# Seven-product sums formed on TensorE, another order of the last pieces, and eight slabs moved

## The chip, the cores and the metric

The kernel is one program on 1 core of one Trainium2 chip. The metric is the device time of one execution in microseconds; three executions of the kernel before had a median of 1919.31 us, from 1918.39 to 1920.64.

## What is computed

One inference step of a decoder layer, for a prompt of 1024 tokens and a group of 8 samples of 4 tokens with the same weights (1056 tokens, width 1024):

```
h     = LN0(x) * (1 + scale1) + shift1             # scale, shift, gate: silu(c) @ w_ada, six vectors per c
proj  = h @ w_in                                   # split among four mixers:
y_a   = S5 state-space scan, gelu, GLU             # "ssm"
y_b   = gated short convolution
y_c   = chunked gated delta rule
y_d   = stick-breaking attention
mixed = sum_n sigmoid(h @ w_gate_n) * (y_n @ w_branch_n)      # w_gate: 1024 x 4096
x     = LN1(alpha * x + (1 + gate1) * (mixed @ w_o))
h2    = LN0(x) * (1 + scale2) + shift2
x     = LN2(alpha * x + (1 + gate2) * ((silu(up_a) * up_b) @ w_down))
```

Inputs, outputs and norms are float32. A large product is formed from f16 halves: each operand is split into a hi and a lo part, and three products hi*hi, hi*lo and lo*hi are accumulated (`mm3`).

## The kernel before, in words

Tokens lie along the free dimension in three blocks of TB = 352 (NTB = 3; HB = 176 is half a block), the width of 1024 as KD = 8 slices on the 128 partitions. The third block carries the 32 sample tokens at its end. The work runs in stages: LN0 and modulation to `h`; projections, attention, convolution and delta rule; the gates; `mixer_out` (w_o, LN1, h2); the feed-forward network; the last down slice with LN2.

A scheduler records the kernel's instructions and fixes one static order for each engine before the program runs. It goes by priorities (streams `sup`, `br`, `lo`, `hot`, which shift an instruction's place) and by a timeline that it simulates. So lines that follow one another in the code stand interleaved with other stages on the engines, and each engine and SP's DMA queue take their instructions strictly in the fixed order.

The stretch of the change:

- `gates(2, ...)`, the third gate, is plain: for each of 8 output slices m it loads 128 x 1024 of weights (`load_w`, transfer on L142, hi split on ScalarE at L108, lo split on GpSimd at L114), forms three token blocks of 24 products `gps<-h,whl`, and beside each the 6 products `gps<-y,wbr` of the branch. ScalarE takes the tanh (`gth`, L1490), VectorE multiplies it with the branch's PSUM (L1494), GpSimd adds the result to `mix` (L1523). PSUM has three banks `gps` for this.
- Between its groups stand *slabs* (`ada_slab`): one slab is one 128-column part of `w_ada`, loaded like a gate weight, and multiplied with the silu of c in 16 tiny products (`gps<-chl,whl`) to one column of modulation `mod` (L294, L295). They are needed only from `mixer_out` on. `A2` is the number of slabs for each m of the third gate; what is left goes to the last gates, spread evenly over their four pairs.
- `ssm` is interleaved with the third gate: matrices by sines and cosines on GpSimd, transfers through HBM (`tt<-kd`, `sy<-yo`, `gx<-sy`), the scan's products (`sps`), gelu, the GLU's 48 products `sps<-yh,whl`, and the split of `y` (L108 on ScalarE, L118 on VectorE).
- `gates7(0, ...)`, the last gates, takes output slices in four pairs and uses a seven-product scheme in place of eight products of half blocks (`seven`; forms in `ORDER7`). Its inputs are slices of h and four sums and differences of slices, `Tf` (in the profile `tf`). `sums7` makes them in six units, for three token blocks and two halves of the width: in one unit 4 adds hi + lo to f32 (L1711, two on VectorE, two on GpSimd), four adds and subtractions on VectorE (L1712, L1715, L1716, L1720) and four splits (L108 on ScalarE, L116 on VectorE). Seven forms of weights are made too (`pair_weights`, L1635 to L1643 on VectorE). The slabs' lo split is on VectorE here (`LA7`, L118). PSUM has five more banks (`gps7`) once `ssm` has released its own.

The last stage goes over four pieces of tokens (`PIECES`). For each piece 8 output slices are multiplied (`gps<-ring`) and added to x (L1966; the sample part with L1971 and L1973), GpSimd sums the slices in `S` (L1547), and `norm` follows: mean by products with a constant matrix (`nps<-S,onesD`, `nps<-x,onesD`), subtract (L186), square on ScalarE (L187), variance in products (`nps<-sq,onesD`) and the root `rs` on ScalarE (L193, L194); `affine` multiplies by rs (L227) and applies gain and offset (L230 on VectorE, L232 on ScalarE). `LV2` says how many halvings of the squares are added on VectorE before the products: 3 for the first two pieces, 0 for the last two. Two DMAs write each piece out. `onesD` products are float32, and each passes TensorE several times.

## Time and profile before

| | |
|---|---|
| median of 3 executions | 1919.31 us |
| lowest, highest | 1918.39, 1920.64 us |
| the profiled execution | 1927.88 us |
| its span in the trace | 1925.8 us |
| mean granted TensorE clock | 0.961 |
| busy: TensorE, VectorE, ScalarE, GpSimd | 90, 67, 50, 50% |

The profile is of one execution that was a little longer than those timed. Its span runs from the first to the last instruction of the trace; all stage times are of that span. Busy times are of one engine; a stage whose engines are all partly idle is bound by waits between them. A granted clock of 1.0 is 2.4 GHz and 0.5 is 1.2 GHz; values between are means over a stretch.

### The profile page before, as it was taken

What the parts mean: (1) busy time and instruction counts of PE and PEld (TensorE: products, weight loads), DVE (VectorE), ACT (ScalarE), POOL (GpSimd) and SP (SyncE); (2) the same over time, 40 slices, a digit from 0 to 9 for tenths busy, and PEclk for the clock granted to TensorE, in tenths of its full rate; (3) what the DMA queues carried; (4) which work ended last, traced back from release to release, by engine and by line L of the source; (5) the groups of instructions that cost most, each with busy time, mean ns of one, the idle gap of its engine ahead of it and who ended that gap; (6) DMA issues with size and microseconds to landing.
All of it is one profiled execution on the core that took longest, in us unless ns stands there. A gap on an engine that the chain in (4) does not pass through costs nothing.

```text
span 1925.8 us, 36541 instructions
## 1 busy us (share of the span) xinstructions
PE 1734.6 (90%) x14985; PEld 1198.5 (62%) x14985; DVE 1297.0 (67%) x2161; ACT 970.8 (50%) x1796; POOL 953.9 (50%) x952
## 2 busy tenths in 40 slices
PE   7899999999899998788689899988999998999896
PEld 3466666656566665556367555556666776767675
DVE  6763777668676765386986479677467657755748
ACT  3642454465554645235664665645445644554434
POOL 1826421222354444744541553278577667675733
PEclk9999999999999999889799999989999999999999
DMA  8222220122311112313232340001121112111112
GB/s 310 75 90 64 73 59 23 49 58 54 96 50 58 62 40 98 73 41 102 77 110 77 129 137 1 1 23 44 48 64 56 48 44 65 56 37 53 50 28 91
DMA packets 63615, 130.60 MB, mean 68 GB/s; under 512 B 16408, under 2 KB 35928, under 8 KB 63192
## 3 DMA queue, kind: packets, MB, share of 16 engines
q1 hardware_dynamic: 61912, 124.07, 20.8%
q0 software_dynamic: 1536, 4.20, 0.7%
q8 instruction: 117, 1.92, 0.4%
q14 instruction: 50, 0.41, 0.1%
HBM read 117.36 MB, written 10.88 MB: 67 GB/s over the span
## 4 chain that ended last, share of the span: by engine, by line
PE 35%; DVE 26%; POOL 12%; ACT 10%; DMA 9%; issue 7%; SPq 1%; another core or an unknown queue 0%; ACTq 0%; DVEq 0%; POOLq 0%
PE gps L87 25%; DMA wraw<-in_w_up 3%; POOL wf L1631 2%; DVE x L1903 2%; POOL whl L1631 2%; DVE ring L116 2%; PE nps L87 1%; DMA wraw<-in_w_down 1%; DVE af L1869 1%; ACT wraw L1622 1%; DVE dacc L758 1%; POOL wraw L1635 1%; PE dp L87 1%; POOL wraw L1638 1%; POOL wraw L1639 1%
## 5 line engine op out<-in xcount | busy, mean ns | idle before, releaser
L87 PEld LDWEIGHTS <-whl 128*128 128x128 f16 x6992 | 623.5, 100 | 386.1 <-issue 74.9
L87 PE MATMUL gps<-h,whl 128*128 128x352 f16 (+1 forms) x4344 | 692.9, 314 | 49.0 <-ACT ct L1683 14.8
L87 PEld LDWEIGHTS <-wf 128*128 128x128 f16 x2232 | 197.7, 99 | 71.6 <-issue 13.8
L1631 POOL TENSOR_TENSOR wf<-wraw,wf 128x512 f16<-128x512 f32 (+1 forms) x102 | 122.8, 1206 | 145.8 <-ACT wf L1630 142.9
L1631 POOL TENSOR_TENSOR whl<-wraw,whl 128x512 f16<-128x512 f32 (+1 forms) x136 | 169.2, 1250 | 47.0 <-ACT whl L1630 46.8
L114 POOL TENSOR_TENSOR whl<-wraw,whl 128x1024 f16<-128x1024 f32 (+1 forms) x66 | 149.1, 2260 | 81.2 <-ACT whl L108 79.2
L105 ACT ACTIVATE wraw<-wraw 128x1024 f32<-128x1024 f32 (+2 forms) x96 | 96.4, 1005 | 127.4 <-DMA wraw<-in_w_gate 40.1
L87 PE MATMUL gps<-tf,whl 128*128 128x352 f16 (+1 forms) x1152 | 141.1, 280 | 18.6 <-ACT ct L1683 6.9
L1622 ACT ACTIVATE wraw<-wraw 128x1024 f32<-128x1024 f32 (+1 forms) x68 | 66.5, 978 | 111.0 <-DMA wraw<-in_w_up 62.2
L1630 ACT ACTIVATE whl<-wraw 128x512 f16<-128x512 f32 (+1 forms) x136 | 79.9, 589 | 78.8 <-POOL wraw L1635 34.5
L87 PE MATMUL gps<-ring,whl 128*128 128x352 f16 (+1 forms) x864 | 103.8, 276 | 13.1 <-DVE x L1903 13.1
L87 PE MATMUL gps<-y,wbr 128*128 128x352 f16 x576 | 105.4, 319 | 8.1 <-DVE gth L1771 3.8
L1680 DVE TENSOR_TENSOR ct<-ct,gps 128x352 f32<-128x352 f32 (+1 forms) x84 | 35.4, 424 | 106.5 <-PE gps L87 90.5
L1523 POOL TENSOR_TENSOR mix<-mix,gth 128x352 f32<-128x352 f32 x48 | 54.0, 1125 | 98.0 <-DVE gth L1494 87.1
L87 PE MATMUL gps<-mix,wo 128*128 128x352 f16 x576 | 88.8, 315 | 5.7 <-DVE gth L1771 3.4
L116 DVE TENSOR_TENSOR ring<-af,ring 128x352 f16<-128x352 f32 (+2 forms) x134 | 82.0, 645 | 7.8 <-ACT ring L108 7.7
L108 ACT ACTIVATE whl<-wraw 128x1024 f16<-128x1024 f32 (+1 forms) x82 | 84.8, 1035 | 4.4 <-DMA wraw<-in_w_ada 3.5
L87 PE MATMUL gps<-h,wf 128*128 128x352 f16 (+1 forms) x624 | 79.4, 283 | 6.6 <-DVE gth L1494 5.5
L87 PEld LDWEIGHTS <-wbr 128*128 128x128 f16 x576 | 56.5, 99 | 39.2 <-issue 10.2
L87 PEld LDWEIGHTS <-wo 128*128 128x128 f16 x576 | 56.7, 99 | 38.6 <-issue 5.9
L108 ACT ACTIVATE ring<-af 128x352 f16<-128x352 f32 (+2 forms) x134 | 52.2, 427 | 46.4 <-DVE af L1869 30.4
L87 PE MATMUL gps<-tf,wf 128*128 128x352 f16 (+1 forms) x528 | 66.6, 283 | 3.8 <-ACT cu L1683 3.6
(625 smaller groups left out, 3381.4 us busy)
## 6 DMA issues: line engine op xcount, KB each, us to landing
wraw<-in_w_up SPq DMA_DIRECT2D x44, 512.0 KB, 3.5
wraw<-in_w_gate SPq DMA_DIRECT2D x32, 512.0 KB, 3.9
wraw<-in_w_ada SPq DMA_DIRECT2D x32, 512.0 KB, 3.5
wraw<-in_w_in SPq DMA_DIRECT2D x20, 512.0 KB, 4.0
wraw<-in_w_down SPq DMA_DIRECT2D x24, 384.0 KB, 3.1
x<-in_xT SPq DMA_DIRECT2D x12, 704.0 KB, 7.7
araw<-in_w_ada SPq DMA_DIRECT2D x16, 512.0 KB, 10.9
wraw<-in_w_branch SPq DMA_DIRECT2D x8, 512.0 KB, 3.5
```

The source lines that it names most:

```text
L87: self.nc.tensor.matmul(out, lhsT=lhsT, rhs=rhs, start=start, stop=stop, skip_group_check=resume)
L105: nc.scalar.activation(src, src, AF.Copy, scale=scale)
L108: nc.scalar.activation(hi, src, AF.Copy, scale=scale)
L114: nc.gpsimd.tensor_tensor(lo, src, hi, op=ALU.subtract)
L116: nc.vector.tensor_tensor(lo, src, hi, op=ALU.subtract)
L758: nc.vector.scalar_tensor_tensor(acc[:, :L], ext[:, k:k + L], wts[:, i, k:k + 1], acc[:, :L], op0=ALU.mult, op1=ALU.add)
L1523: nc.gpsimd.tensor_tensor(o, o, g, op=ALU.add)
L1622: nc.scalar.activation(raw, raw, AF.Copy, scale=SW)
L1630: nc.scalar.activation(hi, src, AF.Copy)
L1631: nc.gpsimd.tensor_tensor(lo, src, hi, op=ALU.subtract)
L1680: add = lambda o, p: nc.vector.tensor_tensor(o, o, p, op=ALU.add)
L1903: nc.vector.scalar_tensor_tensor(x[:, h, z], part(h, z), gate[:, m, 0:1], x[:, h, z], op0=ALU.mult, op1=ALU.add)
```

## The change

- `sums7` is replaced for the last gates by `sums7_pe`. Four sums are formed on TensorE with a 128 x 128 identity (and its negative) in f16 as weights, the hi and lo half of h each being one product of 352 columns. A unit has 12 such products in two PSUM tiles: one for T0, the other for T3, on which T1 and then T2 are accumulated further after the split of the one before. ScalarE's hi split and VectorE's lo split read PSUM. T2 comes out with its sign turned, so its split scales by -1.
- `A2` becomes 2 and `LA7` "pool": eight slabs go from the last gates to the third gate, and the eight that stay have their lo split on GpSimd.
- The sample's block stands second in `PIECES`. The running sum `S` ends one slice earlier, and the mean takes three product terms in place of two, in LN1 and LN2. After the last piece's mean products stand 24 idle products of 352 columns, into a PSUM tile that nothing reads.

```diff
--- before.py
+++ after.py
@@ -32,9 +32,9 @@
 GSPLIT = 4
 G7 = 4
 A3 = 1
-A2 = 1
+A2 = 2
 S7 = 1
-LA7 = "dve"
+LA7 = "pool"
 R7 = (0, 2)
 QT = (0, 1, None, 2, 3, 4, 5, 6, 7)
 CORD = (6, 7, 0, 1, 8, 4, 5, 9)
@@ -44,7 +44,7 @@
 PL1 = ((0, 2), (2,))
 PL2 = (0,)
 LV2 = (3, 3, 0, 0)
-PIECES = ((0, 0, 352), (1, 0, 352), (2, 0, 192), (2, 192, 160))
+PIECES = ((0, 0, 352), (2, 0, 352), (1, 0, 192), (1, 192, 160))
 ALPHA = float(2.0 ** 0.25)
 SW = 64.0
 SA = 16.0
@@ -84,7 +84,7 @@
 
 
     def mm(self, out, lhsT, rhs, start, stop, resume=False):
-        self.nc.tensor.matmul(out, lhsT=lhsT, rhs=rhs, start=start, stop=stop, skip_group_check=resume)
+        self.last_mm = self.nc.tensor.matmul(out, lhsT=lhsT, rhs=rhs, start=start, stop=stop, skip_group_check=resume).ins
 
     def mm3(self, out, w, x, start, stop, resume=False):
         self.mm(out, w[0], x[0], start, False, resume)
@@ -157,7 +157,7 @@
         return ps
 
 
-    def norm(self, X, n, tmp, out=None, levels=3, rs_bufs=1, sq=None, tag=0, preload=True, parts=None, eps=None):
+    def norm(self, X, n, tmp, out=None, levels=3, rs_bufs=1, sq=None, tag=0, preload=True, parts=None, eps=None, warm=None):
 
         nc = self.nc
         out = X if out is None else out
@@ -185,6 +185,12 @@
         for k in (0, 4):
             nc.vector.tensor_tensor(out[:, k:k + 4], X[:, k:k + 4], bc(mean[:, None, :], (P, 4, n)), op=ALU.subtract)
             last = nc.scalar.activation(sq[:, k:k + 4], out[:, k:k + 4], AF.Square)
+        if warm:
+
+            idle = self.gtile()
+            with self.tc.issue_after(self.last_mm):
+                for i in range(warm[1]):
+                    self.mm(idle[:, :TB], warm[0][:, 0:P], warm[0][:, 0:TB], True, True)
         if preload:
             with self.tc.issue_after(last.ins):
                 nc.scalar.preload_act_table_set("natural_log_exp_and_others")
@@ -1543,7 +1549,7 @@
 
         if m == 1:
             self.nc.gpsimd.tensor_tensor(S, X[:, 0], X[:, 1], op=ALU.add)
-        elif 1 < m < KD - 1:
+        elif 1 < m < KD - 2:
             self.nc.gpsimd.tensor_tensor(S, S, X[:, m], op=ALU.add)
 
     def mixer_out(self):
@@ -1590,7 +1596,7 @@
             else:
                 dsq = pw.tile([P, 2 * KD * TB + 2 * 4 * HB], F32, name="dsq", tag="wo")
                 d, sq = dsq[:, :2 * KD * TB].rearrange("p (j k n) -> j p k n", j=2, k=KD)
-            rs = self.norm(x1, TB, tmp, sq=sq, levels=LV1[b], tag=b % 2, preload=b in PL1[0], parts=[S, x1[:, KD - 1]])
+            rs = self.norm(x1, TB, tmp, sq=sq, levels=LV1[b], tag=b % 2, preload=b in PL1[0], parts=[S, x1[:, KD - 2], x1[:, KD - 1]])
             self.affine(x1, rs, self.ln["ln1_ga"], self.ln["ln1_ba"])
             rs = self.norm(x1, TB, tmp, out=d, sq=sq, levels=LV1[b], tag=b % 2, preload=b in PL1[1], eps=self.eps_a)
             self.modulate(d, n0, TB, rs, self.mod[:, 32:40], self.mod[:, 24:32], h2[:, :, :, s])
@@ -1719,6 +1725,23 @@
                 self.split(*T(3), t3)
             nc.vector.tensor_tensor(r21, r21, r22, op=ALU.subtract)
             self.split(*T(2), r21)
+
+    def sums7_pe(self, h, Tf, b, qs):
+
+        part = lambda j, e, i: h[:, j, e::2, b * TB + i * HB:b * TB + (i + 1) * HB][:, qs]
+        T = lambda f: (Tf[:, f, 0, qs, b], Tf[:, f, 1, qs, b])
+        n = 2 * HB
+        view = lambda ps: ps.rearrange("p (q c) -> p q c", c=HB)
+        with self.sup:
+            one, two = self.gtile()[:, :n], self.gtile()[:, :n]
+            for ps, f, sgn, terms in ((one, 0, 1.0, ((0, 0, 1), (1, 0, 0))), (two, 3, 1.0, ((0, 1, 1), (1, 0, 1))),
+                                      (two, 1, 1.0, ((0, 0, 0),)), (two, 2, -1.0, ((1, 1, 0),))):
+                first = f in (0, 3)
+                for t, (neg, e, i) in enumerate(terms):
+                    for j in range(2):
+                        self.mm(view(ps), self.id16[:, neg], part(j, e, i), first and t == 0 and j == 0,
+                                t == len(terms) - 1 and j == 1, True)
+                self.split(*T(f), view(ps), sgn)
 
     @staticmethod
     def forms7(h, Tf):
@@ -1972,7 +1995,8 @@
                                                 bc(gate[:, m, 1:9, None], (P, NB, DS)), op=ALU.mult)
                         nc.vector.tensor_tensor(x[:, npr:], x[:, npr:], t, op=ALU.add)
                     self.running(S, X, m)
-            r = self.norm(X, n, tmp, levels=LV2[i], rs_bufs=2, tag=i % 2, preload=i in PL2, parts=[S, X[:, KD - 1]])
+            r = self.norm(X, n, tmp, levels=LV2[i], rs_bufs=2, tag=i % 2, preload=i in PL2, parts=[S, X[:, KD - 2], X[:, KD - 1]],
+                          warm=(act[0][:, 0], 24) if i == len(PIECES) - 1 else None)
             self.affine(X, r, self.ln["ln2_g"], self.ln["ln2_b"])
             for k in (0, 4):
                 nc.sync.dma_start(O["yT"][:, k:k + 4, s], X[:, k:k + 4])
@@ -2044,9 +2068,12 @@
     B.up_t = g7
     B.gp = B.pool("gps7", bufs=5, space=PSUM)
     Tf = g7.tile([P, 4, 2, 4, NTB, HB], F16, name="tf")
+    B.id16 = g7.tile([P, 2, P], F16, name="id16")
+    for j in range(2):
+        B.nc.vector.tensor_scalar(B.id16[:, j], B.ident, 1.0 - 2 * j, None, op0=ALU.mult)
     for b in range(NTB):
         for q in (0, 2):
-            B.sums7(B.h, Tf, b, g7.tile([P, 8 * HB], F32, name="r7", tag="r7"), slice(q, q + 2))
+            B.sums7_pe(B.h, Tf, b, slice(q, q + 2))
     B.xh7 = B.forms7(B.h, Tf)
     B.sk = B.pool("gate7w", side="right")
     B.ska = B.sk
```

Numbers of lines after the change are 6 or more higher from `norm` on (L1494 becomes L1500, L1635 L1641, L1966 L1989, L227 L233, L230 L236).

VectorE where `ssm` ends, around the splits of `y`; before, with the end of the third unit of the sums (`r_11498`) and the start of the fourth (`r_11515`):

```order
L1720 TENSOR_TENSOR r_11498<-r_11498 128x352
L118 SCALAR_TENSOR_TENSOR y<-gs,y 128x8x128
L118 SCALAR_TENSOR_TENSOR y<-gs,y 128x4x8
L116 TENSOR_TENSOR tf<-r_11498,tf 128x2x176
L1463 SCALAR_TENSOR_TENSOR gs<-gs,gx 128x1088
L295 SCALAR_TENSOR_TENSOR mod<-gps,adat 128x9
L116 TENSOR_TENSOR tf<-r_11498,tf 128x2x176 x3
L1494 SCALAR_TENSOR_TENSOR gth<-gth,gps 128x352
L118 SCALAR_TENSOR_TENSOR y<-gs,y 128x8x128
L118 SCALAR_TENSOR_TENSOR y<-gs,y 128x4x8
L1711 TENSOR_TENSOR r_11515<-h 128x352 x2
```

and now:

```order
L1469 SCALAR_TENSOR_TENSOR gs<-gs,gx 128x1088
L118 SCALAR_TENSOR_TENSOR y<-gs,y 128x8x128
L118 SCALAR_TENSOR_TENSOR y<-gs,y 128x4x8
L1469 SCALAR_TENSOR_TENSOR gs<-gs,gx 128x1088
L1500 SCALAR_TENSOR_TENSOR gth<-gth,gps 128x352
L118 SCALAR_TENSOR_TENSOR y<-gs,y 128x8x128
L118 SCALAR_TENSOR_TENSOR y<-gs,y 128x4x8
L116 TENSOR_TENSOR tf<-gps,tf 128x2x176 x3
L1641 TENSOR_TENSOR wraw<-wraw 128x4x128
L116 TENSOR_TENSOR tf<-gps,tf 128x2x176 x2
```

The adds of the sums are gone, and all the splits of the sums (`tf<-gps`) stand behind both splits of `y`, where before those of two units stood ahead of them.

SP's queue around the transfers of the scan's matrices (`kd`, `tt`) and of its state (`h<-in_st_ssm`); before:

```order
L142 DMA wraw<-in_w_gate 128x1024
L142 DMA wraw<-in_w_ada 128x1024
L1354 DMA kd<-k_10993 128x1x240 x2
L142 DMA wraw<-in_w_gate 128x1024
L1356 DMA tt<-kd 16x16x128 x8
L142 DMA wraw<-in_w_ada 128x1024
L1405 DMA h_11204<-in_st_ssm 128x128
L1418 DMA out_ssm_s<-fs 128x128
L142 DMA wraw<-in_w_gate 128x1024
L142 DMA wraw<-in_w_ada 128x1024
```

and now:

```order
L1360 DMA kd<-k_11201 128x1x240 x2
L142 DMA wraw<-in_w_gate 128x1024
L1362 DMA tt<-kd 16x16x128 x8
L142 DMA wraw<-in_w_ada 128x1024 x2
L1411 DMA h_11412<-in_st_ssm 128x128
L142 DMA wraw<-in_w_gate 128x1024
L1424 DMA out_ssm_s<-fs 128x128
L142 DMA wraw<-in_w_ada 128x1024 x2
L142 DMA wraw<-in_w_gate 128x1024
L1417 DMA out_ssm_p<-fp 128x16
L142 DMA wraw<-in_w_ada 128x1024
L1439 DMA sy<-yo_11431 16x8x136 x8
```

Each slab load (`in_w_ada`) of this stretch has become two, and one stands ahead of the transfer `sy` of the scan's result.

VectorE at the end of the program, where the 352 piece's last passes (128x1408, then 128x352) and the last piece (160 columns) meet; before:

```order
L1971 TENSOR_TENSOR gt<-gps,mod 128x32 x2
L1973 TENSOR_TENSOR x_13853<-x_13853,gt 128x32 x2
L227 TENSOR_TENSOR x_13548<-x_13548,rs 128x1408 x2
L230 TENSOR_SCALAR x_13548<-x_13548,c_ln_g,c_ln_b 128x352 x4
L186 TENSOR_TENSOR x_13853<-x_13853,nps 128x4x160 x2
L227 TENSOR_TENSOR x_13853<-x_13853,rs 128x4x192 x2
L230 TENSOR_SCALAR x_13853<-x_13853,c_ln_g,c_ln_b 128x192 x4
L227 TENSOR_TENSOR x_13853<-x_13853,rs 128x4x160 x2
L230 TENSOR_SCALAR x_13853<-x_13853,c_ln_g,c_ln_b 128x160 x4
```

and now:

```order
L172 TENSOR_TENSOR sq<-sq 128x352
L1989 SCALAR_TENSOR_TENSOR x_13597<-gps,mod,x_13597 128x160 x3
L186 TENSOR_TENSOR x_13597<-x_13597,nps 128x4x160 x2
L233 TENSOR_TENSOR x_13902<-x_13902,rs 128x1408 x2
L236 TENSOR_SCALAR x_13902<-x_13902,c_ln_g,c_ln_b 128x352 x4
L233 TENSOR_TENSOR x_13597<-x_13597,rs 128x4x192 x2
L236 TENSOR_SCALAR x_13597<-x_13597,c_ln_g,c_ln_b 128x192 x4
L233 TENSOR_TENSOR x_13597<-x_13597,rs 128x4x160 x2
L236 TENSOR_SCALAR x_13597<-x_13597,c_ln_g,c_ln_b 128x160 x4
```

The last piece's subtract with its mean (`x<-x,nps 128x4x160`) has moved ahead of the passes of the 352 piece, and the sample's instructions (`gt`) are no longer among these.

## Rows read from the trace of the kernel before

**Rows 1.** Windows by stage: us; busy us (instructions) per engine; TensorE's granted clock; DMA share; GB/s.
```profile
700.00:876.20 176.20, 148.58 (x1212) 99.63 (x1210) 97.64 (x215) 72.07 (x147) 92.46 (x85) 0.91 0.24 66
876.20:956.80 80.60, 58.60 (x425) 37.52 (x424) 70.92 (x79) 46.30 (x71) 41.29 (x30) 0.83 0.27 87
956.80:1020.00 63.20, 52.62 (x482) 38.07 (x481) 55.51 (x85) 42.68 (x85) 30.96 (x24) 0.89 0.37 118
1020.00:1069.80 49.80, 49.80 (x479) 37.16 (x476) 27.74 (x59) 22.35 (x48) 2.53 (x1) 1.00 0.16 53
```

**Rows 2.** Timeline of TensorE, 876 to 957: start, us, operation, count [idle before, releaser].
```profile
878.40 3.74 PE L87 MATMUL gps<-h,whl 128*128 128x352 f16 x24
881.98 1.06 PE L87 MATMUL gps<-y,wbr 128*128 128x352 f16 x6
...
918.58 6.66 PE L87 MATMUL gps<-h,whl 128*128 128x352 f16 x24 [5.22 <-ACT gth L1490]
...
936.15 0.89 PE L87 MATMUL gps<-h,wf 128*128 128x176 f16 x5 [5.54 <-DVE gth L1494]
```

**Rows 3.** VectorE's lines, 880 to 1080: shapes, count | busy us, mean ns | idle before.
```profile
L118 DVE SCALAR_TENSOR_TENSOR whl<-wraw,whl 128x1024 f16<-128x1024 f32 x16 | 23.3, 1456 | 0.0
...
L116 DVE TENSOR_TENSOR tf<-r,tf 128x352 f16<-128x352 f32 x24 | 16.4, 692 | 0.0
...
L1711 DVE TENSOR_TENSOR r<-h 128x352 f32<-128x352 f16 x12 | 14.1, 1214 | 0.0
...
L1712 DVE TENSOR_TENSOR r<-r 128x352 f32<-128x352 f32 x6 | 5.9, 979 | 0.0
...
L1715 DVE TENSOR_TENSOR r<-r 128x352 f32<-128x352 f32 x6 | 3.9, 646 | 0.2
...
L1716 DVE TENSOR_TENSOR r<-r 128x352 f32<-128x352 f32 x6 | 3.6, 594 | 0.0
...
L1720 DVE TENSOR_TENSOR r<-r 128x352 f32<-128x352 f32 x6 | 3.1, 517 | 0.1
```

**Rows 4.** Tile `gth`: count, ns min/median/max, first and last start, shapes.
```profile
L1494 DVE SCALAR_TENSOR_TENSOR gth<-gth,gps x48: 494/514/523, 557.5 to 946.7; 128x352 f32<-128x352 f32 x48
...
L1519 DVE TENSOR_TENSOR gth<-gth,mix x24: 510/522/2448, 982.9 to 1073.2; 128x352 f32<-128x352 f32 x24
```

**Rows 5.** Timeline of VectorE, 876 to 958.
```profile
883.67 2.89 DVE L1711 TENSOR_TENSOR r<-h 128x352 f32<-128x352 f16 x2
...
927.48 5.33 DVE L118 SCALAR_TENSOR_TENSOR y<-gs,y 128x1024 f16<-128x1024 f32 x2 [3.08 <-ACT y L108]
...
948.26 2.25 DVE L1711 TENSOR_TENSOR r<-h 128x352 f32<-128x352 f16 x2
```

**Rows 6.** TensorE's lines from 876.2, from 956.8 and from 1020, one of each.
```profile
L87 PE MATMUL sps<-yh,whl 128*128 128x272 f16 x48 | 6.6, 279 | 1.1 <-POOL whl L114 0.5 <-ACT whl L108 0.4
...
L87 PE MATMUL gps<-chl,whl 128*128 128x18 f16 x113 | 4.4, 172 | 2.6 <-DVE mod L295 2.6
...
L87 PE MATMUL gps<-chl,whl 128*128 128x9 f16 x83 | 2.8, 169 | 0.0
```

**Rows 7.** GpSimd's lines, 780 to 880.
```profile
L114 POOL TENSOR_TENSOR whl<-wraw,whl 128x1024 f16<-128x1024 f32 x8 | 17.9, 2235 | 5.1 <-ACT whl L108 5.1
```

**Rows 8.** Timeline of TensorE at the end.
```profile
1904.32 0.86 PE L87 MATMUL nps<-sq,onesD 128*128 128x352 f32 x2 [1.54 <-DVE sq L172]
...
1914.27 4.09 PE L87 MATMUL nps<-sq,onesD 128*128 128x160 f32 x16 [4.30 <-ACT sq L187]
```

**Rows 9.** Timeline of VectorE at the end.
```profile
1907.65 3.51 DVE L227 TENSOR_TENSOR x<-x,rs 128x1408 f32<-128x1408 f32 x2 [1.16 <-ACT rs L194]
1911.09 1.57 DVE L230 TENSOR_SCALAR x<-x,c_ln_g,c_ln_b 128x352 f32<-128x352 f32 x4
1912.58 1.54 DVE L186 TENSOR_TENSOR x<-x,nps 128x640 f32<-128x640 f32 x2
```

**Rows 10.** Waits of SP's queue: us in total, times, longest.
```profile
SPq L142 <- POOL whl L114: 420.0, 40, 27.1
```

## The prediction

> **What bounds the kernel now.** I read the page's busy shares first (TensorE 90% of the span, no other engine above 67%), then its slices, of which those around 880 to 1020 us are among the few where TensorE works under nine tenths, and then cut that stretch into stages. In the stage table [rows 1] the reader is to see where TensorE is not the limit. From 876.2 us (the end of the S5 scan's products) to 956.8 us (the first product on the sums) TensorE works 58.6 of 80.6 us at a granted clock of 0.83, while VectorE works 70.9. In the first two weight pairs of the last gates (956.8 to 1020) it is 52.6 of 63.2 at 0.89, VectorE 55.5. In the last two pairs (1020 to 1069.8) nearly the same products take 49.8 us with TensorE busy throughout, clock 1.00, VectorE only 27.7. So the region is bound by VectorE until about 1020 and by TensorE afterwards. TensorE's timeline [rows 2] shows single waits: 5.22 us at 918.58 and 5.54 at 936.15, for gate values that stood on ScalarE and VectorE behind the strided splits of `y` and the sums [rows 5]. What VectorE did in 880 to 1080 us stands in its lines [rows 3]: the five lines of the sums, 14.1 + 5.9 + 3.9 + 3.6 + 3.1 = 30.6 us; the lo split of the slabs (L118 `whl`), 23.3; the lo split of the sums (L116), 16.4. At the program's end the bound is a chain: mean, subtract, square, variance, rs, two last passes [rows 8, 9].
>
> **The change part by part.**
>
> *Sums on TensorE.* VectorE loses 30.6 us of adds [rows 3], GpSimd the other 12 adds of L1711; ScalarE and VectorE keep 24 splits each, now from PSUM. A VectorE instruction with one PSUM and one SBUF source took 0.514 us in the median and at most 0.523 (L1494, 48 times); one with two SBUF sources 0.522 in the median and up to 2.448 (L1519) [rows 4]. So I take 0.51 a split: 24 x (0.692 - 0.51) = 4 us more off VectorE. TensorE gets 72 products of 352 columns. In [rows 2] 24 such products start at 878.40 and what follows them at 881.98: 0.149 each, 10.7 us in all.
>
> *Slabs.* Eight leave the last gates for the third gate, and the eight that stay have their lo split on GpSimd, so VectorE loses all 23.3 us of L118 `whl`. With the sums that is 30.6 + 23.3 + 4 = 58 us, of 154 that it works between 876.2 and 1069.8 [rows 1]; TensorE's idle time in the two stages is 22.0 + 10.6. The eight moved slabs cost GpSimd 2.24 us each ahead of the scan [rows 7], a transfer each on SP's queue, and TensorE 16 tiny products each: 83 of them took 2.8 us [rows 6], so 0.54 a slab.
>
> The Trainium skill, page "SBUF — State Buffer", section "SBUF: two separate sides", says that VectorE and GpSimd share one port pair as an exclusive lock: a VectorE instruction with two SBUF inputs and a GpSimd instruction that reads SBUF keep each other out for a whole instruction. The 0.523 against 2.448 of [rows 4] agrees with it. It speaks against the split's move to GpSimd, where a slab holds the pair for 2.24 us. If each of the eight made one two-input instruction of VectorE wait 2.448 - 0.522 = 1.9 us with TensorE behind it, 15 us would come back and the time would be 1913; I leave it out, as VectorE has room in this stage once it is relieved.
>
> *Step 1, up to the end of the scan's products.* Bounds: 0 (GpSimd works 92.5 of the 176.2 us before 876.2 [rows 1], so the splits may fit in its gaps) and 17.9 us (eight in series [rows 7]). In the new order gate 4's weights stand behind four more slab splits, 4 x 2.24 = 9 us, and the scan's products with `U` stand on TensorE behind that gate's groups. The scan has a slower chain of its own at that time, transfers through HBM. I take +3, near the low end, since GpSimd has 84 us of gaps.
>
> *Step 2, from there to the first product on the sums.* The new order has on TensorE in it: nine gate groups of 24 + 6 products, 9 x 30 x 0.149 = 40.2; six slabs, 3.3; the 48 products of the GLU, 6.6 [rows 6]; 66 of the 72 identity products, 9.8; the first forms that need only h, 24 products of 352 and 24 of 176 columns, 3.6 + 1.8 = 5.4. Sum 65.3 us at full clock. VectorE, which had five of the six pairs of L1711 in this stage (the first at 883.67, the fifth at 948.26 [rows 5]), loses some 5/6 of 30.6, so it works 45 us there and is no limit. What remains are the splits of `y` (5.33 us on VectorE, after a wait of 3.08 for ScalarE's half [rows 5]) and that T1 and T2 follow T3 on one bank. I allow 5 us for these: 70 against 80.6, so -10.6. Bounds: 65.3 (no wait) and 80.6 (no gain).
>
> *Step 3, the last gates.* The first two pairs have the products of the last two, and 113 slab products against 83 [rows 6]. With VectorE relieved they should go at the pace of the last two, 49.8 for 63.2; I leave 1.2 us for half clock at the start: 51, so -12.2. Bounds: -13.4, and -6, some half of it, if only the idle time that the sums' adds and slab splits make goes and the clock stays low. Of the 12 slabs in both parts six are gone, 6 x 0.54 = 3.2 us, half of it taken off the path: -1.5. Together -13.7.
>
> *Step 4, the two norms.* The first norm has one GpSimd add fewer and one more f32 product a norm, under 0.5 us of TensorE (two of 352 columns took 0.86 [rows 8]): 0, bounds -1 and +1. In the last norm three things move. The last piece loses the sample's small VectorE instructions, and its subtract (1.54 us) goes ahead of the passes of the 352 piece, where 3.51 + 1.57 us stood in front of it [rows 9]. Its squares now stand behind four affines on ScalarE, and rs of the third piece behind those squares. And 24 idle products run before the variances: the last variance took 4.09 us, 16 passes of 160 columns at 256 ns [rows 8]; at double pace it would take 2. I add this up to +0.3 us, bounds -3 (variance 2 us less, subtract 1 us earlier) and +3 (two affines of the 352 piece on the path, 1.5 us each as L230's four).
>
> *Sum.* +3 - 10.6 - 13.7 + 0.3 = -21 us. The profiled execution took 1927.88 us (span 1925.8 and 2.08 around it), so by its own time 1907. It stands 8.57 us above the median of the runs, 1919.31; the same 21 off that gives **1898 us**.
>
> **The rivals.**
>
> *(a) The sums become a chain of their own.* T1 and T2 are accumulated on T3's bank, and each step waits until both splits have read it, about 0.5 + 0.5 + 0.3 = 1.3 us, 4.5 a unit with T0. These splits stand on VectorE behind both splits of `y`, which ended at 932.8 [rows 5], 936 with step 1. Six units one after the other end at 963; overlapped by half, at 950. For it: that order. Against it: gate groups stand between, and two tiles alternate. At 960 step 1 and 2 are +3 together, and with -13.7 it is about **1908**.
>
> *(b) Slower: the moved slabs delay the scan.* A slab's transfer waits on SP for a raw buffer that GpSimd must free, 420.0 us in 40 such waits, 10.5 each [rows 10], and the scan's transfers (tt, the state, sy and gx) stand behind it in the same queue. The new order has extra slabs ahead of three of these: 3 x 10.5 = 31 us on the chain that sets the scan's end. With -24 for the other steps: **1926**. It decides once the scan's end is later by more than 24 us. Against it: GpSimd's gaps, and that such waits are mostly of slabs issued early with nothing urgent behind them.
>
> *(c) TensorE alone bounds the region.* Step 1 costs 0, step 2 takes 65.3 (-15.3), step 3 -13.4 - 3.2, step 4 -2: -34, **1885**.
>
> **How the numbers follow.** Forecast 0.60, (a) 0.21, (b) 0.09, (c) 0.10. The forecast's own range is 1890 to 1904. The range reaches to (c) and past (a), to step 3 at its lower bound with nothing else gained (1919.3 - 6): 1884 to 1914; left out are (b) and the ends. What a measurement of this kernel can tell from no change is about 0.2%, 3.8 us. (b) is slower by more, 0.09; of (a), 0.06 may fall within it, with step 3 at its bound and step 1 dearer; the other 0.85 is faster.
>
> **What would show it.** Step 1: the scan's last small product ends by 881. Step 2: the first `tf` product starts 67 to 72 us later, VectorE works under 50 us in between, and its splits from PSUM take 0.5 us each. Step 3: the first two pairs take about 51 us, TensorE idle under 2, clock 0.95 or more. Step 4: the last variance takes some 2 us and the end keeps its distance from the last down product. The forecast is wrong if the scan's end moves by more than 10 us, if the first `tf` product stays at 955 or later, or if VectorE's two-input instructions in the last gates stretch to a mean above 1 us.

## The result and the profile after

The changed kernel took 1937.64 us in the median of five runs (1936.83 to 1941.56), the kernel before 1919.31: a ratio of 1.0096 with a 95% interval of 1.0084 to 1.0108. It is slower by 1%; the forecast was 1898.

The profile of before that the prediction started from was of a long execution. A second one of the same kernel had a span of 1912.5 us; most of the 13 us between them lie ahead of the stages of the change and behind the gates. The stages are set side by side with this second profile. They are cut at five of TensorE's products: the first product of the delta rule's norm (`nth`), the scan's last small product, the first product on the sums (`tf`), the first on `mix`, the first of the last down slice. Columns: window; busy us (instructions) of TensorE, its weight loads, VectorE, ScalarE, GpSimd; granted clock; DMA share; GB/s. Windows of the kernel before:

```profile
618.60:869.75 251.15, 219.36 (x2215) 147.11 (x2212) 150.46 (x330) 113.26 (x224) 130.43 (x119) 0.93 0.22 63
869.75:950.40 80.65, 57.60 (x425) 37.02 (x424) 70.75 (x79) 46.25 (x71) 41.28 (x30) 0.83 0.27 87
950.40:1065.90 115.50, 101.37 (x958) 74.33 (x956) 86.71 (x147) 68.02 (x136) 36.30 (x26) 0.95 0.27 88
1065.90:1837.00 771.10, 711.53 (x5688) 514.92 (x5688) 517.97 (x836) 408.11 (x798) 488.43 (x416) 0.98 0.18 54
1837.00:1912.50 75.50, 61.32 (x486) 47.08 (x483) 53.56 (x99) 27.32 (x44) 24.69 (x28) 0.95 0.19 65
```

The same windows of the changed kernel:

```profile
620.50:883.00 262.50, 226.69 (x2258) 152.38 (x2255) 155.24 (x334) 126.63 (x239) 142.60 (x123) 0.88 0.24 73
883.00:975.80 92.80, 72.57 (x548) 47.79 (x548) 53.35 (x64) 62.11 (x100) 50.19 (x34) 0.87 0.31 97
975.80:1075.00 99.20, 95.49 (x862) 70.79 (x859) 58.36 (x104) 53.04 (x106) 28.51 (x20) 0.98 0.14 47
1075.00:1860.30 785.30, 716.57 (x5694) 517.78 (x5695) 518.46 (x840) 412.10 (x802) 487.88 (x414) 0.98 0.17 53
1860.30:1936.10 75.80, 64.93 (x518) 49.13 (x515) 53.04 (x99) 26.87 (x44) 22.64 (x24) 0.96 0.19 65
```

Stage by stage the change gives +11.4, +12.2, -16.3, +14.2 and +0.3 us. The last gates gained what was forecast and a little more. The scan's end, the stretch behind it and the stages behind the gates (the mixer's output and the feed-forward network) took more than that back.

*The scan.* TensorE's timeline (start, us, operation, count, idle before and releaser), changed kernel:

```profile
860.69 0.97 PE L87 MATMUL sps<-hi,cai 64*128 64x137 f32 x10 [1.43 <-DVE hi L1226]
861.59 0.53 PE L87 MATMUL gps<-chl,whl 128*128 128x9 f16 x15
...
862.46 0.82 PE L87 MATMUL sps<-hr,car 64*128 64x137 f32 x2
...
882.18 0.82 PE L87 MATMUL sps<-hr,car 64*128 64x137 f32 x2
```

and the same place in the second profile of before:

```profile
853.28 1.57 PE L87 MATMUL sps<-hi,cai 64*128 64x137 f32 x10 [2.75 <-DVE hi L1220]
854.78 3.43 PE L87 MATMUL gps<-h,whl 128*128 128x352 f16 x15
858.05 0.40 PE L87 MATMUL sps<-U,tt 128*128 128x137 f32 x2
858.38 0.50 PE L87 MATMUL sps<-hr,car 64*128 64x137 f32 x2
```

Before, 15 wide f16 products of a gate stood between TensorE's wait and the scan's float32 products, and a pair of these took 0.50 us at a granted clock of 1.00. In the changed order the scan follows a wait with only narrow products between, and each pair `hr` takes 0.82 from the first to the last, at a granted clock of 0.50. A set (`U`, `hr`, `hi`) starts every 1.96 us (862.46, 864.42) in place of every 1.09; eleven sets make 9.6 of the 11.4 us.

*From the scan to the first product on the sums.* TensorE, changed kernel:

```profile
913.81 1.10 PE L87 MATMUL sps<-yh,whl 128*128 128x272 f16 x8
...
943.26 1.92 PE L87 MATMUL gps<-h,id 128*128 128x352 f16 x6 [12.29 <-DVE tf L116]
```

VectorE there, answering to [rows 5]:

```profile
938.09 4.76 DVE L118 SCALAR_TENSOR_TENSOR y<-gs,y 128x1024 f16<-128x1024 f32 x2 [4.38 <-ACT y L108]
942.54 1.09 DVE L116 TENSOR_TENSOR tf<-gps,tf 128x352 f16<-128x352 f32 x2
```

and the transfers of the GLU's weights on SP's queue, first changed, then before (first profile):

```profile
901.26 4.36 SPq L142 DMA_DIRECT2D wraw<-in_w_glu  x2
```

```profile
853.00 0.33 SPq L142 DMA_DIRECT2D wraw<-in_w_glu  x1
...
860.23 0.38 SPq L142 DMA_DIRECT2D wraw<-in_w_glu  x1
```

Before, these transfers were issued 16 to 23 us ahead of the scan's last product (876 us); now 18 us behind it (883), after SP had waited 9.6 us for a GpSimd split (`whl`, L114) that frees a raw buffer. The GLU's products start at 913.81, so the second split of `y` ends at 942.9, and behind it on VectorE stand the splits of the sums, for which TensorE waits 12.29 us.

*The end.* The last variance, 16 products as in [rows 8], in the second profile of before and in the changed kernel, and two of VectorE's last passes in the latter:

```profile
1902.44 2.41 PE L87 MATMUL nps<-sq,onesD 128*128 128x160 f32 x16 [2.73 <-ACT sq L187]
```

```profile
1925.15 2.44 PE L87 MATMUL nps<-sq,onesD 128*128 128x160 f32 x16 [0.88 <-ACT sq L187]
```

```profile
1918.19 1.55 DVE L186 TENSOR_TENSOR x<-x,nps 128x640 f32<-128x640 f32 x2 [1.99 <-PE nps L87]
1919.66 3.16 DVE L233 TENSOR_TENSOR x<-x,rs 128x1408 f32<-128x1408 f32 x2
```

The subtract went ahead of the 352 piece's passes, as the order said. The variance takes 2.44 us; that is less than the 4.09 of the first profile of before, but the second has 2.41 without idle products. The stage is 75.8 us against 75.5.

### The profile page after: what moved, and what is told of

It reads as the page before. It is cut to its first block, busy times and chain, and to the rows that moved or that the text cites. A ratio compares the mean times of both kernels' runs of the same rounds, so it can differ in the third digit from the quotient of the medians.

```text
span 1936.1 us, 36698 instructions
## 1 busy us (share of the span) xinstructions
PE 1755.0 (91%) x15095; PEld 1214.2 (63%) x15095; DVE 1256.5 (65%) x2111; ACT 989.0 (51%) x1814; POOL 965.6 (50%) x949
## 4 chain that ended last, share of the span: by engine, by line
PE 41%; DVE 23%; POOL 11%; ACT 9%; DMA 9%; issue 5%; SPq 1%; ACTq 0%; DVEq 0%; POOLq 0%
PE gps L87 30%; DMA wraw<-in_w_up 3%; POOL wf L1637 2%; DVE x L1926 2%; DMA wraw<-in_w_down 1%; PE nps L87 1%; POOL whl L1637 1%; PE sps L87 1%; PE dp L87 1%; DVE ring L116 1%; PE x L87 1%; POOL whl L114 1%; DVE dacc L764 1%; ACT wraw L1628 1%; PE z L87 1%
## 5 line engine op out<-in xcount | busy, mean ns | idle before, releaser
L114 POOL TENSOR_TENSOR whl<-wraw,whl 128x1024 f16<-128x1024 f32 (+1 forms) x82 | 188.0, 2295 | 109.3 <-ACT whl L108 97.9
L1637 POOL TENSOR_TENSOR whl<-wraw,whl 128x512 f16<-128x512 f32 (+1 forms) x136 | 161.0, 1191 | 39.9 <-ACT whl L1636 35.0
L105 ACT ACTIVATE wraw<-wraw 128x1024 f32<-128x1024 f32 (+2 forms) x112 | 113.1, 1011 | 123.5 <-DMA wraw<-in_w_ada 40.6
L87 PE MATMUL gps<-h,wf 128*128 128x352 f16 (+1 forms) x624 | 76.6, 276 | 0.0
```

The costliest lines, as they stand in the source:

```text
L87: self.last_mm = self.nc.tensor.matmul(out, lhsT=lhsT, rhs=rhs, start=start, stop=stop, skip_group_check=resume).ins
L105: nc.scalar.activation(src, src, AF.Copy, scale=scale)
L114: nc.gpsimd.tensor_tensor(lo, src, hi, op=ALU.subtract)
L1637: nc.gpsimd.tensor_tensor(lo, src, hi, op=ALU.subtract)
```

## The experiments

Ratios are to the kernel before, run beside each on the same chip. "First three stages" are the windows above.

**The two kernels again.** No edit.

> The kernel before once more, for a second profile of it. The first profiled execution took 1927.88 us against a median of 1919.31, so some 8 us of its trace are its own. If the extra time lies in the stages that are compared, this profile shows the first product on the sums some us earlier than 956.8 and the last stage's start earlier than 1848.9; if it lies ahead of 700 us, only the whole trace is shifted.

> The changed kernel once more, for a second profile. In the first its scan's products ran through one stretch of 23.9 us at half clock (the kernel before has none there) and three more such stretches of 3.4 us stood in the feed-forward stage. If they belong to the kernel they come again at the same places, the scan's end is 262 us after the delta rule's norm and the time is 1935 to 1941; if they were chance, the scan's end is at 251 and the time below 1930.

> The changed kernel as it is, beside the next one on the same chip. Two looks at it gave 1937 (with a stretch of 23.9 us at half clock over the scan's products) and 1922 (without it). Theory C1 (the stretch comes in most runs): 1934 to 1940 here. Rival C2 (it is rare): 1920 to 1925.

Before: 1914.57. The changed kernel: 1922.02 once, and in six more runs 1936.66 (1.0091, 1.0063 to 1.0119), of which five were 1933.6 to 1941.7 and one 1923.5. So its twelve runs fall into two groups, ten at 1933 to 1942 and two at 1922 to 1924; of the fast group there is one profile. In the profile of the 1922 the scan's pairs run at full clock:

```profile
860.29 0.97 PE L87 MATMUL sps<-hi,cai 64*128 64x137 f32 x10
...
861.58 0.48 PE L87 MATMUL sps<-U,tt 128*128 128x137 f32 x2
861.99 0.50 PE L87 MATMUL sps<-hr,car 64*128 64x137 f32 x2
```

The order of the products is the same, but here TensorE did not wait ahead of these rows, and the granted clock is 1.00 over the scan. The first stage is then 251.9 us (+0.8 to before), the second 90.2. The half clock over the scan accounts for the 10.6 us by which the first stage differs between the two profiles.

**The parts alone.** Each takes one part of the diff over to the kernel before: `sums7_pe`; `A2 = 2` with `LA7 = "pool"`; or `PIECES`, the third mean term and the 24 idle products.

```diff
-            B.sums7(B.h, Tf, b, g7.tile([P, 8 * HB], F32, name="r7", tag="r7"), slice(q, q + 2))
+            B.sums7_pe(B.h, Tf, b, slice(q, q + 2))
```

> Only the sums on TensorE; slabs, pieces and norms as before. Theory A (the moved slabs delay the scan and leave more gate groups after it, and the splits of y come into the open by that): the scan's end stays near 876, the first two pairs of the last gates take about 50 us for 63, and the time is 1906 to 1914. Theory B (the sums' own chain, identity products and splits behind both splits of y, costs more than the adds did): the scan's end stays, but the first tf product comes 8 to 16 us later, and the time is 1918 to 1930.

> Only the eight slabs moved and the lo split of the others on GpSimd; sums on VectorE as before. Theory A: the scan's end is 8 to 12 us later as in the changed kernel, the last gates lose some of it again as VectorE has 23 us of splits less, and the time is 1922 to 1932. Theory B: the scan may be later, but gate groups and sums fill the time, and it is 1910 to 1920.

> Only the pieces' order, the third mean term in the two norms, and the idle products. The changed kernel's trace has 20.9 us from the last down product to the end against 23.0 before, so 1917 to 1918 if nothing else follows from this part. The rival is that this part also moves the order of mixer and feed-forward stage, where the changed kernel lost some 9 us against the first profile: then 1922 to 1928.

Sums: 1911.28, 0.9969 (0.9955 to 0.9983). Slabs: 1939.54, 1.0122 (1.0102 to 1.0142). End: 1917.34, 1.0000 (0.9988 to 1.0011). The slabs make the change slow, the sums are the only gain, the end by itself is nothing. The first three stages are 252.8, 80.4 and 98.5 us with the sums, 251.1, 92.7 and 107.3 with the slabs. The slabs' time lies above both ranges that were expected, and the scan's end is not later: in this profile, of the fastest of the five runs, the scan runs at full clock. Against the second profile of before its 20.5 us are 12.1 in the second stage, -8.2 in the last gates, 8.4 behind them, 4.6 in the last stage and 3.6 ahead of the first.

**The changed kernel without the slabs' move, and with the split on GpSimd alone.**

```diff
-A2 = 2
-LA7 = "pool"
+A2 = 1
+LA7 = "dve"   # the second kernel: "pool"
```

> The changed kernel with the slabs as before (one for each m, lo split on VectorE); sums on TensorE, pieces, norms and idle products stay. If the parts add, sums 6 us and the end 0 give 1909 to 1913. If the scheduler's order of the feed-forward stage, which is another in each kernel, takes more of it back: 1915 to 1920.

> As the kernel without the moved slabs, but the lo split of the 16 slabs of the last gates on GpSimd. If GpSimd's splits keep two-input instructions of VectorE waiting there (the shared port of the forecast), the last gates take 3 to 8 us longer than without and the time is 1913 to 1919; if VectorE has room there, as its idle time says, the difference is within 2 us.

1911.55 (0.9971, 0.9960 to 0.9982) and 1918.77 (1.0010, 0.9997 to 1.0023): the split of 16 slabs on GpSimd costs 7.2 us. The last gates take it, 98.5 and 105.7 us:

```profile
953.80:1052.30 98.50, 96.09 (x958) 72.49 (x956) 64.76 (x124) 55.79 (x114) 18.36 (x14) 1.00 0.26 91
```

```profile
951.10:1056.80 105.70, 100.24 (x977) 74.31 (x974) 64.64 (x112) 68.33 (x129) 49.33 (x30) 0.97 0.28 90
```

TensorE's idle time there grows by 3 us, and its clock is 0.97 in place of 1.00, which is some 4 us more of busy time. VectorE's lines (count; busy, mean ns; idle before), split on VectorE:

```profile
L1525 DVE TENSOR_TENSOR gth<-gth,mix 128x352 f32<-128x352 f32 x22 | 14.2, 669 | 0.0
L1794 DVE SCALAR_TENSOR_TENSOR gth<-ct,gps 128x352 f32<-128x352 f32 x23 | 11.1, 514 | 5.5 <-ACT ct L1781 5.5
...
L1641 DVE TENSOR_TENSOR wraw<-wraw 128x512 f32<-128x512 f32 x2 | 1.4, 686 | 1.2 <-POOL wf L1637 1.2
```

and on GpSimd:

```profile
L1525 DVE TENSOR_TENSOR gth<-gth,mix 128x352 f32<-128x352 f32 x22 | 18.6, 874 | 0.0
...
L1794 DVE SCALAR_TENSOR_TENSOR gth<-ct,gps 128x352 f32<-128x352 f32 x23 | 11.2, 515 | 7.2 <-ACT ct L1781 7.2
...
L1641 DVE TENSOR_TENSOR wraw<-wraw 128x512 f32<-128x512 f32 x2 | 3.2, 1607 | 0.0
```

These instructions with both sources in SBUF stretch, from 669 to 874 ns and from 686 to 1607; the one with a PSUM source keeps 514. Not all of the first kind do: L1649 stays at 680 ns, and L1645 took 1630 in both kernels. The Trainium skill, page "SBUF — State Buffer", section "SBUF: two separate sides", has this as an exclusive port pair of VectorE and GpSimd, and the rows shown agree.

**The GLU's weights loaded early, into tiles of their own.** Transfer and split stand at the start of `ssm`, on the changed kernel:

```diff
+        pgl = self.pool("glu_w")
+                raw = pgl.tile([P, 256], F32, name="graw%d" % i)
+                nc.sync.dma_start(raw, I["w_glu"][i])
+                hl = pgl.tile([P, 2, 256], F16, name="gwhl%d" % i)
+                self.split(hl[:, 0], hl[:, 1], raw, SW, lo_eng="pool")
...
-            w = self.load_w(I["w_glu"][i])
+            w = gw[i]
```

> The changed kernel, with the GLU's weights loaded into two small tiles of their own at the start of the scan's stage, so that they no longer queue behind slabs and gate weights. Theory A1 (the moved slabs cost by what they push back in the shared weight buffers, the GLU's weights above all, and with it y and the sums): the GLU comes some 20 us after the scan's end in place of 31, the first tf product 80 to 84 us after it in place of 92.8, and the time is 1922 to 1930. Rival A2 (they cost by the gate groups that wait longer for PSUM and by the half clock in the scan): the time stays at 1933 to 1940.

1923.46 (1.0035, 1.0016 to 1.0055). The transfer's row, and the second stage:

```profile
734.58 5.12 SPq L1210 DMA_DIRECT2D graw<-in_w_glu  x2
```

```profile
888.10:965.80 77.70, 63.38 (x493) 42.06 (x493) 48.57 (x59) 53.72 (x86) 40.00 (x26) 0.90 0.28 90
```

The second stage falls from 92.8 to 77.7 us with the slabs still moved. So the 12 us that it had grown by came from the GLU's weights, which were late behind the slabs. The run takes away the place in the queue and the wait for a raw buffer together and does not part the two. The scan still ran at half clock (first stage 267.2). Here 15 wide products stood ahead of it again, and its first set ran at full clock; the fall came behind a wait inside the run:

```profile
869.12 0.51 PE L87 MATMUL sps<-U,tt 128*128 128x137 f32 x2 [1.63 <-ACT yo L1444]
869.57 0.82 PE L87 MATMUL sps<-hr,car 64*128 64x137 f32 x2
```

**Idle products at the scan.** Their output is overwritten. First one f16 product of 352 columns ahead of each of 16 sets, then 20 together ahead of the main run and 8 in its middle; the last kernel has these 28 and the early GLU weights.

```diff
-                ps = psum("y")[:, 0:137]
+                pf = psum("y")
+                for _ in range({5: 20, 10: 8}.get(g, 0)):   # first kernel: one for each g
+                    self.mm(pf[:, 0:TB], self.h[:, 0, 0, 0:P], self.h[:, 0, 0, 0:TB], True, True)
+                ps = pf[:, 0:137]
```

> The changed kernel with one idle f16 product of 352 columns ahead of each of the scan's 16 sets of products, 16 x 0.149 = 2.4 us of work that is thrown away. C1 (the scan's float32 products leave TensorE at half clock when it comes to them after a wait, which the slabs' order brings about, since the gate group that ran into the scan before is now done earlier): the stretch goes or becomes short, and the time is 1920 to 1926, whatever the kernel above shows. C2 (the clock there has nothing to do with what runs): the time is that of the kernel above and 2.4 us more.

> The changed kernel with 20 idle f16 products of 352 columns right ahead of the scan's main run of products and 8 in its middle, 28 x 0.149 = 4.2 us of work thrown away. In the kernel before, 13 f16 products of a gate group stand right ahead of that run and it goes at full clock. If the order ahead of the scan brings the half clock about, the stretch of 23.9 us goes and the time is 1924 to 1930 in nearly all executions; if not, it is 1937 and 4 to 8 more.

> The changed kernel with the GLU's weights loaded early and the same 28 idle products. With early weights alone most executions took 1920 to 1929 and one 1911, and the profile had the stretch at half clock over the scan. If the idle products lift it, 1912 to 1918 in nearly all executions; if not, 1926 to 1932.

1939.49 (1.0113, 1.0093 to 1.0132), 1931.02 (1.0066, 1.0052 to 1.0079) and 1917.55 (1.0015, 0.9999 to 1.0030). With single products the pairs stay at 0.82:

```profile
860.05 0.31 PE L87 MATMUL sps<-h 128*128 128x352 f16 x1
860.20 0.39 PE L87 MATMUL sps<-U,tt 128*128 128x137 f32 x2
860.52 0.82 PE L87 MATMUL sps<-hr,car 64*128 64x137 f32 x2
```

With 20 together they run at 0.50:

```profile
858.18 4.82 PE L87 MATMUL sps<-h 128*128 128x352 f16 x20
862.84 0.40 PE L87 MATMUL sps<-U,tt 128*128 128x137 f32 x2
863.17 0.50 PE L87 MATMUL sps<-hr,car 64*128 64x137 f32 x2
```

The 28 gain about 6 us on either kernel by the medians, 4 to 6 by the ratios, after what they take themselves (4.82 us for the first 20); on the kernel with early weights the two intervals overlap. The single products gained nothing, as the rival that the clock has nothing to do with what runs had said; the 20 and the 8 speak against that rival. In all four profiles with the scan at half clock TensorE had waited 1.4 to 1.6 us ahead of the run or inside it, and no dense run of products stood behind the wait. Where one did (15 wide products before, 20 idle ones here), or where no such wait stood, the scan ran at full clock.

**The eight slabs in the earlier gates** (`A3 = 2`, `A2 = 1`, `LA7 = "dve"`), ahead of the third gate.

> Sums, pieces and norms of the changed kernel, and the eight slabs moved, but to the gates ahead of the third gate (two for each m there, one in the third gate; lo split of the last gates' slabs on VectorE). If moving slabs costs by what stands in the buffers and queues beside the scan (A1), this one pays little: the last gates gain 2 to 3 us by eight slabs less, 1908 to 1914. If any slab that goes forward delays the scan's matrices and transfers, the scan's end is 5 to 12 us later: 1917 to 1925.

1933.57 (1.0088, 1.0072 to 1.0104). It missed both ranges: the scan's end is 11.6 us later again, as the second of them had it, but the time is 9 us above it. The scan's first transfer, without the slabs' move and in this kernel:

```profile
800.21 1.86 SPq L1360 DMA_DIRECT2D kd<-k  x2
```

```profile
818.51 3.08 SPq L1360 DMA_DIRECT2D kd<-k  x2
```

Against the stage's start (620.7 and 626.1) it is 12.9 us later, behind slabs and their raw buffers on the queue or behind GpSimd, which makes `k`; the run doesn't part these two. In this kernel the half clock lies over other products, and the scan's pairs take 0.50.

**Early GLU weights without the slabs' move**: on the changed kernel with `A2 = 1` and `LA7 = "dve"`, on before with the sums, and on before alone.

> Sums on TensorE, pieces and norms of the changed kernel, slabs as before, and the GLU's weights loaded early into their own tiles. If the GLU's weights are late in the order without the moved slabs too, the stage from the scan's end to the first tf product falls from 79.5 to some 74 us and the time from 1911.5 to 1905 to 1909. If they are on time there (the GLU stood 14 us after the scan's end without them), it stays within 2 us of 1911.5.

> The kernel before with the sums on TensorE and the GLU's weights loaded early; pieces, norms and slabs as before. The pieces and norms made no difference alone (1.000) and none beside the sums (1911.3 and 1911.6), so 1904 to 1908 as with them. If they matter in this combination, through the order of the later stages, 1909 to 1914.

> The kernel before with the GLU's weights loaded early, and nothing else. Its sums on VectorE bound the stage until 1020 us, so the GLU's place should not matter: 1915 to 1918. If the GLU was late there too and VectorE has room, it gains the 4 to 6 us that the kernel with the sums on TensorE gained: 1910 to 1913.

**1905.75 us (0.9937, 0.9921 to 0.9952)**, faster than both kernels; 1909.68 (0.9962, 0.9948 to 0.9977); 1918.22 (1.0014, 1.0002 to 1.0026). On before alone the early weights gain nothing. With the sums alone they gain 1.6 us more than the sums, inside the noise; with the sums and the new end they gain 5.8. So the end, worth nothing alone, may be worth some 4 us here (the two intervals just touch): the last stage takes 75.8 us with it, 79.8 without. In the 13 profiles of kernels with the new end that stage takes 75.7 to 76.6 us, in the six without it 75.4 to 80.1. The first of the three, by stage:

```profile
619.20:868.90 249.70, 218.12 (x2218) 146.56 (x2216) 147.82 (x330) 114.94 (x228) 134.93 (x121) 0.94 0.23 67
868.90:945.00 76.10, 62.48 (x493) 41.63 (x493) 52.77 (x64) 50.45 (x84) 38.60 (x25) 0.91 0.29 93
945.00:1043.60 98.60, 96.12 (x957) 72.49 (x955) 65.39 (x124) 56.69 (x117) 18.55 (x16) 1.00 0.28 91
1043.60:1828.50 784.90, 712.58 (x5695) 515.32 (x5696) 516.14 (x840) 411.04 (x801) 483.71 (x414) 0.98 0.17 54
```

**A delay behind the gates.** That first kernel is 22.3 us ahead of the one before at the first product on `mix` and gives 13.8 back by the last down slice (784.9 for 771.1). 100 idle products, overwritten by the first real one, delay these stages; the instructions in them keep nearly their order on every engine.

```diff
+                if b == 0 and m == 0:
+                    for i in range(100):
+                        self.mm(ps[:, :TB], wo[:, 0, 0, 0:P], self.mix_hl(KD - 1, NTB - 1)[0], True, True)
```

> The kernel of sums on TensorE, slabs left in place and early GLU weights (1905.75 us, mixer and feed-forward 784.9 us from the first product on mix to the last down slice), with 100 idle products of 352 columns put on TensorE right ahead of the first product on mix; the first real product overwrites what they leave. They delay everything behind the gates by 100 x 0.149 = 14.9 us and leave the order of the instructions in the stages behind nearly as it is. If the stage grew because it is reached earlier (something in it, weights or their conversion, has its own timetable that an earlier start does not move), it shrinks back from 784.9 to 771 to 776 once it starts later, and the time rises by 1 to 6 us only, to 1907 to 1912. If it grew because the scheduler's new order of its instructions is a worse one, it stays at 783 to 787 and the time rises by the whole 14.9, to 1919 to 1922.

1908.00 us (0.9966, 0.9952 to 0.9981), 2.3 us more than without the products, or 5.6 by the two ratios. The stage, and the idle products in it, in a profile of the fastest of the ten runs (1902.22):

```profile
1037.00:1823.90 786.90, 723.94 (x5795) 524.85 (x5796) 520.67 (x839) 413.14 (x801) 482.99 (x414) 0.98 0.16 53
1037.00:1051.90 14.90, 14.81 (x100) 9.73 (x101) 8.36 (x7) 5.42 (x8) 9.28 (x4) 1.00 0.47 163
```

Without the 14.9 it is 772.0: in this profile 12.9 of the 14.9 us come back, and by the times 9 to 13. So a later start of the stage by itself moves its end little.

The time on the clock is not what counts, though: the changed kernel reaches the first product on `mix` at 1075.0, 9 us later than before (1065.9), and still takes 785.3 us behind it. Nor is it the order of the instructions: the kernel with the new end alone has the same order of TensorE's 5693 products in this stage as the changed kernel. Its last gates and this stage:

```profile
948.40:1064.90 116.50, 101.14 (x958) 75.04 (x956) 87.88 (x147) 67.82 (x136) 36.69 (x26) 0.96 0.27 87
1064.90:1839.10 774.20, 709.23 (x5695) 514.05 (x5695) 516.64 (x837) 409.54 (x798) 478.07 (x413) 0.99 0.17 54
```

That is 774.2 us for 785.3 with one order. What goes with the long stage is a short stay in the last gates. From the first product on the sums to the last down slice it is 886.6 us before, 884.5 in the changed kernel, 883.5 in the fastest one and 885.3 with the delay; over all 19 profiles it is 880 to 895, while the last gates alone take 96 to 123.

## Why the prediction was wrong

**Step 1, the scan's end: +3 forecast, +11.4 measured.** The bounds of 0 to 17.9 held it, but by another cause than the splits on GpSimd. In the profile at full clock it is +0.8, so GpSimd's gaps did take the extra splits; the rest is half clock over the scan. The prediction took the scan's products at the pace of before and did not ask what would stand ahead of them. In the changed order the gate's products had moved off that place, and a wait of 1.4 us of TensorE just ahead went with half clock over the whole run; in the profiled run of the fast group, with the same order, there was no such wait. Loading the GLU's weights early does not remove this; dense products between the wait and the run do.

**Step 2, -10.6 forecast, +12.2 measured: the step that failed most.** Two things are in it. The sum put 5 us for waits; without the slabs' move (79.5 us in this stage against 80.7) TensorE still waits 13.3 us on `tf`, and with early weights 12.1 (76.1 us). So rival (a), the sums as a chain behind both splits of `y`, was what the sums really did here, and the relief of VectorE (70.8 to 52.8 us busy) bought 1 to 5 us, not 10. On top of it the moved slabs put the GLU's weights behind them in SP's queue and its raw buffers, 15 us by the run that takes just this away. That is rival (b)'s mechanism at another place: I weighed the scan's transfers against the slabs and forgot the next small transfer in that queue. In the changed kernel the scan's first transfer was at 805.80 us, 185 after the stage's start, against 179 before; the rival's 31 us did not come.

**Step 3, the last gates: right for the stage.** From the first product on the sums to the first on `mix` it is 99.2 for 115.5 us, -16.3 against -13.7. TensorE is busy 95.5 of 99.2 at a clock of 0.98. The sums alone do it (98.5); the slabs alone give 8 us here. But the stages behind gave nearly all of it back, as told below.

**The lock left out of the sum: present.** Its price was put at 15 us if it counted, and left out since VectorE would have room. With 16 slabs on GpSimd it measures 7.2 us, of which some 4 are TensorE's clock. In the last gates of the changed kernel L1525 has a mean of 850 ns, under the 1 us named as the sign, which was set too high.

**Step 4: right in size, in part by luck.** +0.3 us in the last stage, and a ratio of 1.0000 alone. From the end of the last down product to the end it is 20.9 us for 21.6, but the down products end 1.0 us later in the stage. The sum knew the variance only at 4.09 us; in the profile that it is compared with it took 2.41 already, and the kernels that keep the old end vary there by 4.7 us.

**What no step had: 14 us behind the gates.** The sum took every microsecond saved at the gates as saved at the end. It isn't: what the last gates gained (-16.3) the mixer's output and the feed-forward network lost again (+14.2), and counted from the first product on the sums their end is where it was, within 2.1 us. The run with the new end alone shows that the new order of these stages does 3 us of it at most (774.2 us with the same order); the delay shows that time put in ahead of them comes back for the most part. Small waits grow throughout, mostly for ScalarE and VectorE: TensorE is idle for 72.3 us of these stages in the fastest kernel, 63.0 with the delay, 59.6 before. Which resource sets that time (the weights' transfers, their conversion on ScalarE and GpSimd, a buffer count) no run here tells, and it stays open.

In sum, against the second profile of before: 8.4 us on step 1, 22.8 on step 2, -2.6 on step 3, 14.2 behind the gates and 1.9 ahead of the first stage are 44.7. The forecast was added to the runs' median, 4.7 us above that profile; the rest, 40.0, is within 0.4 the miss from 1898 to 1937.6.

## What to carry to other kernels

When work is moved ahead of a stage on a queue that issues in order, list every transfer behind it to the next few stages, small ones too, and give each the new wait: 15 us came from two loads of weights that no step had priced. Look at what stands directly ahead of a run of narrow float32 products on TensorE, since a wait there may decide their clock. A gain at one stage counts at the end only if the stages behind it do not give it back; a delay of known length put ahead of them, and a kernel with the same order there and a slower stage ahead, tell that.

## What the runs showed of the hardware

The scan's float32 products kept one clock from their second set to the end of their run of 12 to 22 us: 0.50 us a pair at a granted clock of 1.00, or 0.82 at 0.50, in the same kernel in different runs. They went to the lower one behind waits of TensorE of 1.4 to 1.6 us. One f16 product between sets did not lift it to 2.4 GHz, 20 in a row ahead of the run did. And a VectorE instruction on SBUF alone took up to 2.3 times as long beside GpSimd's splits (686 to 1607 ns), while one with a PSUM source went from 514 to 515 ns.
